# Handing a transformer layer's token mixer over to its mixture of experts: order, places, weight ring and last stage

## The chip, the cores and the metric

One core of one Trainium2 chip runs the whole layer in one launch. The metric is the device time of that launch in microseconds; 1,024 tokens of width 1,024, all in 32-bit floats.

## What is computed

The layer has two halves. The token mixer (differential attention and gated linear attention, then two branch projections and an output projection) is added to its input and normalized. The second half, around which the change lies, is a mixture of 32 experts in 4 groups:

```python
u = _modulate(x, sh2, sc2)
g_idx = argmax(u @ w_rg + b_rg)                    # one of 4 groups per token
top_v, top_i = lax.top_k(e_in, 2)                  # two of its 8 experts
weights = softmax(top_v) * g_w
h = silu(xblk @ wg[e]) * (xblk @ wu[e])            # per expert; 1024 -> 512, twice
yb = h @ wd[e]                                     # 512 -> 1024
y = segment_sum(yb * buf_w)                        # two rows per token, weighted
x = _layer_norm(DEEPNORM_ALPHA * x + g2 * y, ln2_g, ln2_b)
```

## The kernel before

**Router and mixer's end.** `mixer` ends with the output projection of token tiles 4 to 7. For each 128-token tile, `out_tile` (L1550) transposes the residual row, forms the router's logits, and normalizes twice through `norm` (L1524); the second call writes the row that the experts will read, and the logits' last line (L1573) stands behind that call. `Moe.route` and `Moe.forced` (L191) then pick the two experts of each token and, for expert 0 alone, the list of its tokens (`idx` column 0, L205 to L207).

**Three kinds of experts.** Expert 0 is fixed: 128 rows in plain 32-bit, `full32` (L520). The other 31 are sorted by their token counts in `place` (L222): the eight fullest are heavy (`Big`, 256, 192 or 128 rows; each weight half is split by ACT and DVE into two parts, L360 and L361, and multiplied in three terms), the 23 others are light (`Small`, 64 or 32 rows; plain 32-bit weights, no split). `place` gives each token's row position (`posi`, L289), the sorted expert numbers (`eidi`, L249, read by SP as addresses of the weights) and, by 16 matmuls on one-hot tables (L308), the token list of all blocks (`idx`, L309). In the code it stands behind `full32`.

**Weights.** Each expert has six halves of 1 MB (gate, up and down, two each), loaded by SP in order (`load`, L337, L349) into a ring of eight buffers `raw0` to `raw7`. A heavy half leaves its buffer when it is split, a light half when TensorE has multiplied it. The first four ring buffers take the fixed expert's gate and up halves, its down halves go into two spare tiles (L365 to L367). The ring is the first pool on the left side of memory, where the router's constants and the mixer's tiles lay; the pool `pxc`, with the row scales `g2` and the small tables of `place`, is on the right side (L371).

**Order.** `ORDER` (L46) is a string of 140 steps written by hand: H is the next step of the heavy experts (four up steps, a turn, a down step each: 48 steps), L the next one of the light experts (two up steps, the down step of the expert before, a turn: 92 steps). TensorE keeps that order; the splits of a heavy step are issued two steps ahead (L738 to L745). Rows of tokens come by indirect gathers on POOL (`gather`, L388): tag `xg` and tag `xgl` have one buffer each. Before the first step the two row blocks of the first heavy expert are gathered and turned, then the first light expert's (L728 to L732).

**Last stage.** After a loop over overflow blocks (L763, its count is read by every engine) the eight token tiles are finished in the order 4, 5, 6, 7, 0, 1, 2, 3 (L794): two gathers on POOL per tile (`y_rows`, L784, four tiles ahead, 6 buffers each), TensorE adds the two weighted rows through diagonal matrices, tiles 4 to 7 with the residual as a third product by the identity and ACT for the sum (L809), tiles 0 to 3 with the residual added by DVE (L811). Then the mean (L812), ACT's squares (L813), variance (L814), a power on POOL (L815), and two DVE passes (L816, L817) before the store (L818). The residual rows of tiles 0 to 3 are loaded by SP near the end of the steps (L657 to L660).

## Time and profile before

| | |
|---|---|
| Time, median of 3 runs | 2019.95 us (2017.43 to 2022.34) |
| Profiled execution: its time | 2018.9 us |
| its span, first to last instruction | 2017.1 us |
| mean granted TensorE clock | 0.971 |
| PE busy | 1878.1 us (93%) |
| DVE busy | 1154.8 us (57%) |
| ACT busy | 851.0 us (42%) |
| POOL busy | 222.8 us (11%) |
| HBM read, written | 359.64 MB, 72.89 MB |

The span is cut in stages further below. All times of rows are microseconds from the start of the span. PE is TensorE's matmul, DVE is VectorE, ACT is ScalarE, POOL is GpSimd, SP is the engine that issues most loads. L327 is the line of a helper through which all matmuls of the experts go, L330 that of the transposes; the tile names tell them apart (`tru` rows of tokens, `pf` and `ypf` the fixed expert's up and down products, `ptb` the token lists, `pg` and `pu` heavy up, `ps` light up, `yp` down, `fs` the last stage). A 32-bit matmul shows as two records, so counts of its instructions are twice the number in the code.

### The profile page before, as it was taken

How to read it: one execution, taken by the hardware profiler on the slowest of the kernel's cores; microseconds unless marked ns; L12 is line 12 of the kernel's file. 1: busy time of each engine (PE TensorE's matmuls, PEld its weight loads, DVE VectorE, ACT ScalarE, POOL GpSimd, SP SyncE). 2: the span in 40 equal slices, each digit the busy share in tenths (PEclk: the TensorE clock that was granted, in tenths of full speed). 3: DMA queues.
4: the chain of work that ended last, by engine and by line, in shares of the span. 5: the costliest groups of instructions: out<-in, count | busy, mean ns of one | idle time of the engine just before them, and what ended most of it. 6: DMA issues, size and time to landing. Idle time of an engine off the chain costs nothing. (4 is left out here: it accounts for less than half of the span.)

```text
span 2017.1 us, 29004 instructions
## 1 busy us (share of the span) xinstructions
PE 1878.1 (93%) x11019; PEld 1369.9 (68%) x11019; DVE 1154.8 (57%) x2123; ACT 851.0 (42%) x1434; POOL 222.8 (11%) x345
## 2 busy tenths in 40 slices
PE   6999999999999999999998999995989898899886
PEld 4777777777777777777776788884646545466542
DVE  7755276576567655887633576788423324335555
ACT  5321166566557655566563343532212212223422
POOL 1131200000000000000010100101101111011115
PEclk9999999999999999999999999997899999999988
DMA  7896482311221322122158844634799999999976
GB/s 279 227 247 216 137 284 94 102 61 58 95 88 41 102 78 83 45 85 75 58 161 291 262 153 136 207 113 174 301 422 418 410 422 414 421 405 422 396 317 242
DMA packets 142668, 430.59 MB, mean 213 GB/s; under 512 B 20102, under 2 KB 49414, under 8 KB 116416
## 3 DMA queue, kind: packets, MB, share of 16 engines
q1 hardware_dynamic: 99168, 350.60, 47.0%
q0 software_dynamic: 42880, 77.97, 12.1%
q8 instruction: 87, 1.43, 0.3%
q14 instruction: 53, 0.43, 0.1%
q10 hardware_dynamic: 480, 0.16, 0.0%
HBM read 359.64 MB, written 72.89 MB: 214 GB/s over the span
## 5 line engine op out<-in xcount | busy, mean ns | idle before, releaser
L327 PE MATMUL ps<-rawr,xT 128*32 128x256 f32 (+1 forms) x1120 | 133.6, 455 | 15.2 <-DMA rawr<-in_wu 9.3
L1152 DVE CUSTOM_DVE_ANT_0 t<-sc,B 128x256 f32<-128x256 f32 (+7 forms) x128 | 95.8, 754 | 63.8 <-PE sc L1149 58.7
L361 DVE TENSOR_TENSOR wL<-rawr,wH 128x1024 fp32r<-128x1024 f32 x96 | 113.4, 1220 | 19.5 <-ACT wH L360 18.9
L923 PE MATMUL v<-wv,uH 128*128 128x512 f32 x256 | 103.4, 414 | 5.8 <-DVE veL L868 4.5
L327 PEld LDWEIGHTS ps<-rawr,xT 128*32 128x32 f32 (+1 forms) x1120 | 50.2, 119 | 85.1 <-issue 43.9
L1154 ACT ACTIVATE t<-t,nm 128x256 f32<-128x256 f32 (+7 forms) x128 | 98.7, 772 | 17.1 <-DVE nm L1152 16.8
L360 ACT CAST wH<-rawr 128x1024 fp32r<-128x1024 f32 x96 | 95.5, 1048 | 22.7 <-DMA rawr<-in_wd 9.0
L885 PE MATMUL g<-uH,wH_g 128*128 128x512 f32 x256 | 102.3, 400 | 1.8 <-DVE kz L1111 1.8
L574 ACT ACTIVATE sg<-ps 64x256 f32<-64x256 f32 (+1 forms) x23 | 11.0, 479 | 218.6 <-PE ps L327 218.6
L924 PE MATMUL v<-wv,uL 128*128 128x512 f32 x256 | 102.7, 401 | 0.0
L925 PE MATMUL v<-wv,uH 128*128 128x512 f32 x256 | 102.3, 400 | 0.0
L886 PE MATMUL g<-uL,wH_g 128*128 128x512 f32 x256 | 101.9, 398 | 0.0
L887 PE MATMUL g<-uH,wL_g 128*128 128x512 f32 x256 | 101.7, 397 | 0.0
L576 DVE TENSOR_TENSOR h<-ps,sg 64x256 f32<-64x256 f32 (+1 forms) x23 | 12.7, 554 | 115.8 <-ACT sg L574 115.8
L867 ACT CAST aH<-pta 128x512 fp32r<-128x512 f32 (+1 forms) x80 | 43.4, 543 | 71.2 <-PE pta L1173 70.8
L1147 PE MATMUL sc<-sk,sq 128*128 128x512 f32 (+2 forms) x192 | 70.1, 369 | 1.2 <-DVE nm L1152 0.3
L868 DVE TENSOR_TENSOR aL<-pta,aH 128x512 fp32r<-128x512 f32 (+1 forms) x80 | 50.7, 633 | 34.8 <-ACT aH L867 33.8
L1159 DVE SCALAR_TENSOR_TENSOR t<-t,rsum,t 128x128 f32<-128x128 f32 (+3 forms) x64 | 52.2, 816 | 27.3 <-ACT t L1158 27.0
L923 PEld LDWEIGHTS v<-wv,uH 128*128 128x128 f32 x256 | 49.1, 194 | 25.8 <-DVE veL L868 6.7
L1149 PE MATMUL sc<-kz,sq 128*128 128x512 f32 (+2 forms) x192 | 65.8, 349 | 0.0
L327 PE MATMUL yp<-rawr,hT 128*32 128x256 f32 (+1 forms) x560 | 63.6, 450 | 0.9 <-DMA rawr<-in_wd 0.8
L598 POOL DMA_DIRECT2D yd<-ys x66 | 34.2, 525 | 241.7 <-DVE ys L596 168.4
(534 smaller groups left out, 5110.9 us busy)
## 6 DMA issues: line engine op xcount, KB each, us to landing
rawr<-in_wg SPq DMA_DIRECT2D x62, 1024.0 KB, 15.6
rawr<-in_wu SPq DMA_DIRECT2D x62, 1024.0 KB, 12.9
rawr<-in_wd SPq DMA_DIRECT2D x62, 1024.0 KB, 15.0
war<-in_w_ada SPq DMA_DIRECT2D x32, 512.0 KB, 5.8
yd<-o SPq DMA_DIRECT2D x24, 512.0 KB, 6.5
wa<-in_w_ada_sc SPq DMA_DIRECT2D x8, 1024.0 KB, 9.0
wvr<-in_wv SPq DMA_DIRECT2D x32, 256.0 KB, 3.6
wr_g<-in_wgt SPq DMA_DIRECT2D x16, 512.0 KB, 4.7
```

Source lines behind the costliest of these rows:

```text
L327: return tc.keep_in_program_order(nc.tensor.matmul(*a, **kw))
L360: S.copy(H[:, s], raw[:, s])
L361: V.tensor_tensor(L[:, s], raw[:, s], H[:, s].bitcast(F32), op=ALU.subtract)
L885: MM(ps, H[:, k, :], uH[k][:, s], start=k == 0, stop=False)
L886: MM(ps, H[:, k, :], uL[k][:, s], start=False, stop=False)
L887: MM(ps, L[:, k, :], uH[k][:, s], start=False, stop=k == 7)
L923: MM(ps, uH[k][:, t], wv[c][k][:, 0, :], start=k == 0, stop=False)
L924: MM(ps, uL[k][:, t], wv[c][k][:, 0, :], start=False, stop=False)
L925: MM(ps, uH[k][:, t], wv[c][k][:, 1, :], start=False, stop=k == 7)
L1147: mm = MM(ps[:, k0:k1], q, SK[:, c, k0:k1], start=True, stop=False)
L1152: V.tensor_tensor_reduce(out=t[:, :n], in0=ps[:, :n], in1=B[:, 1024 - n:1024], scale=1.0, scalar=3e38, op0=ALU.add, op1=ALU.min, accum_out=nm)
L1154: S.activation(t[:, :n], t[:, :n], AF.Exp, bias=nm, scale=-1.0, accum_out=rsum[:, c:c + 1])
```

## The change

- `ORDER` begins with light steps and ends with three of them; it has the same 48 heavy and 92 light steps.
- `forced` merges the last two small DVE operations into one; `norm` gets a hook, through which the logits' last line is issued ahead of the second pass over the row.
- `place` becomes a generator that is begun before `full32`. Its matmuls for the token lists come out of its middle and are put behind the fixed expert's up products, ahead of its Silu. The sorted numbers (`eqc`, `eid`, `eidi`) move behind `posi`.
- The pool `pxc` becomes the first pool on the left side, and the ring lies behind it. The fixed expert's down halves are loaded after the gather of its rows; a one-element memset on POOL, queued behind the gather, touches each of the two tiles first, and `g2_loads` follows.
- The fixed expert's turned rows are copied by ACT instead of DVE.
- The first light expert's rows are gathered and turned first; the second row block of the first heavy expert is turned at its first step.
- Last stage: all 16 gathers are issued at once into 8 buffers each, the residual rows of tiles 0 to 3 are loaded on POOL's queue behind the first eight gathers; only the first tile takes the residual through TensorE and ACT, the other seven through DVE; the power on POOL becomes a square root on ACT and a reciprocal on DVE.

The moved `eqc` block (L242 to L249 before) stands unchanged behind L289, and `epsf` is a constant column set by a memset.

```diff
-ORDER = ("HHLLHLLLHLLLLHLLLLHLLLLHHLLLLLHHLLLLL"
-         "LLHHLLLLHHLLLLLHHLLLLLLLHHLLLLHHLLLLL"
-         "HHLLLLLLLHHLLLLHHLLLLHHLLLLHHLLLLLHHH"
-         "HLLLLLHHLLHHHHLHHHLLHHHLLLHLH")
+ORDER = ("LLHLLLLLLHHHLLLLLLLHHLLLLLHHLLLLHHL"
+         "LLLLLLHHLLLHHLLLLHHLLLLLLLHHLLLLHHH"
+         "LLLLLLHLLLLHHLLLLLHHHHLLLLLLLHHHLLL"
+         "LLHHHLLHHHLLHHHLLLLLHHHLLHHHHLLHLLL")
...
-        V.tensor_tensor(self.idxf, pf, self.idxf, op=ALU.add)
-        if i1 == 8:
-            V.tensor_scalar(self.idx[:, 0:NF], self.idxf, float(EMPTY), None, op0=ALU.add)
+        if i1 < 8:
+            V.tensor_tensor(self.idxf, pf, self.idxf, op=ALU.add)
+        else:
+            V.scalar_tensor_tensor(self.idx[:, 0:NF], pf, float(EMPTY), self.idxf, op0=ALU.add, op1=ALU.add)
...
         ptb = pps.tile([128, W], F32, tag="tr", name="ptb")
+        ohs = []
         for h in range(2):
             oh = pr.tile([128, 8, 128], F32, tag="xH", name=f"oh{h}", bufs=3)
+            ohs.append(oh)
...
-            for q in range(8):
-                nc.tensor.matmul(ptb, oh[:, q, :], rb[:, 8 * h + q, :], start=h + q == 0, stop=h + q == 8)
-        V.tensor_scalar(self.idx[:, NF:], ptb[:, NF:], float(EMPTY), None, op0=ALU.add)
...
         V.tensor_copy(self.ovei, ove[0:1, :])
+        yield
+        for h in range(2):
+            for q in range(8):
+                self.tc.keep_in_program_order(nc.tensor.matmul(ptb, ohs[h][:, q, :], rb[:, 8 * h + q, :],
+                                                               start=h + q == 0, stop=h + q == 8))
+        V.tensor_scalar(self.idx[:, NF:], ptb[:, NF:], float(EMPTY), None, op0=ALU.add)
+        yield
...
+        pc = wx.enter_context(tc.tile_pool(name="pxc", bufs=1, reuse_waits="tile"))
         praw = wr_.enter_context(tc.tile_pool(name="raw", bufs=1, reuse_waits="tile"))
...
-        def load(e, which, nm, pool=None, halves=(0, 1), fixed={}):
+        def load(e, which, nm, pool=None, halves=(0, 1), fixed={}, touch=False):
...
+                if touch:
+                    nc.gpsimd.memset(raw[0:1, 0:1], 0.0)
...
+        f0 = [load(0, j, "f0") for j in (0, 1)]
         sp = [phl.tile([128, 2048], F32, tag=t, name=f"rawf0s{j}") for j, t in enumerate(("wL", "wH"))]
-        f0 = [load(0, 0, "f0"), load(0, 1, "f0")]
-        f0.append(load(0, 2, "f0", fixed={0: sp[1], 1: sp[0]}))
...
-        def x_small(u, tag, xg=None):
+        def x_small(u, tag, xg=None, copy=V.tensor_copy):
...
-                V.tensor_copy(T[:, s, :], pt)
+                copy(T[:, s, :], pt)
...
-        def full32(raws, T, ydst):
+        def full32(raws, T, ydst, mid):
...
                 ps.append(p)
+            mid()
             h = px.tile([128, 512], F32, tag="sg", name="hf")
...
-        T0 = x_small(0, "xT64", xg0)
+
         with tc.issue_after(self.last_gather.ins):
+            f0.append(load(0, 2, "f0", fixed={0: sp[1], 1: sp[0]}, touch=True))
             g2_loads()
-        full32(f0, T0, yd[0:128, :])
-        self.place(pc, px, ptr)
+        place = self.place(pc, px, ptr)
+        next(place)
+        full32(f0, x_small(0, "xT64", xg0, S.copy), yd[0:128, :], lambda: next(place))
...
             xl2.append(rows)
-            for i in range(0, 4, 2):
-                t = phl.tile([128, 2, 1024], F32, tag="wL", name=f"x1f{i}")
-                nc.sync.dma_start(t, x1d[i * 128:(i + 2) * 128, :].rearrange("(c p) d -> p c d", p=128))
-                xl2.append(t)
...
+        lights[0].fetch()
         fetch(expert(0), 0)
+        lights[0].rows()
         fetch(expert(0), 1, "xgl")
-        for j in range(2):
-            turn_rows(expert(0), j)
-        lights[0].fetch()
+        turn_rows(expert(0), 0)
...
             if i >= 0 and order[i] is not None:
+                if order[i] == 0:
+                    turn_rows(expert(0), 1)
                 hs[order[i]][2]()
...
-                y = pf.tile([128, 1024], F32, tag=f"y{j}", name=f"y{j}_{i}", bufs=6)
+                y = pf.tile([128, 1024], F32, tag=f"y{j}", name=f"y{j}_{i}", bufs=8)
...
+        for i in order:
+            y_rows(i)
+            if i == 7:
+                for q in range(0, 4, 2):
+                    t = phl.tile([128, 2, 1024], F32, tag="wL", name=f"x1f{q}")
+                    nc.gpsimd.dma_start(t, x1d[q * 128:(q + 2) * 128, :].rearrange("(c p) d -> p c d", p=128))
+                    xts[q], xts[q + 1] = t[:, 0], t[:, 1]
         for n, i in enumerate(order):
-            for m in order[n:n + 4] if n == 0 else order[n + 3:n + 4]:
-                y_rows(m)
...
-            if i > 3:
+            if n == 0:
                 terms.insert(0, (ident, xts[i]))
...
-            if i > 3:
+            if n == 0:
                 S.activation(y0, ps, AF.Identity, accum_out=sm[:, 0:1])
...
-            V.tensor_scalar(sm[:, 1:2], sm[:, 1:2], 1.0 / 1024, EPS, op0=ALU.mult, op1=ALU.add)
-            nc.gpsimd.tensor_tensor(sm[:, 2:3], sm[:, 1:2], mhalf, op=ALU.pow)
+            S.activation(sm[:, 2:3], sm[:, 1:2], AF.Sqrt, bias=epsf, scale=1.0 / 1024)
+            V.reciprocal(sm[:, 2:3], sm[:, 2:3])
...
-    def norm(src, dst, tmp, junk, g, b, nmu, sm, acc=None):
+    def norm(src, dst, tmp, junk, g, b, nmu, sm, acc=None, mid=lambda: None):
...
         G.tensor_tensor(sm[:, 1:2], sm[:, 0:1], mhalf, op=ALU.pow)
+        mid()
         V.scalar_tensor_tensor(dst, tmp, sm[:, 1:2], b, op0=ALU.mult, op1=ALU.add, accum_out=acc)
...
-        norm(z, u2, u2, xa, rows["sc2"], rows["sh2"], sm[:, 5:6], sm[:, 6:8])
-        V.scalar_tensor_tensor(lg, lg, sm[:, 7:8], rc[:, 2, :], op0=ALU.mult, op1=ALU.add)
+        norm(z, u2, u2, xa, rows["sc2"], rows["sh2"], sm[:, 5:6], sm[:, 6:8],
+             mid=lambda: V.scalar_tensor_tensor(lg, lg, sm[:, 7:8], rc[:, 2, :], op0=ALU.mult, op1=ALU.add))

```

## Rows read from the trace of the kernel before

**Rows 1.** Windows of stages: length, busy PE, PEld, DVE, ACT, POOL; clock, DMA share, GB/s.

```profile
1320.00:1375.00 55.00, 54.22 (x292) 44.66 (x291) 45.55 (x132) 19.00 (x30) 5.06 (x9) 1.00 0.17 63
...
1475.00:1945.00 470.00, 425.29 (x2666) 260.49 (x2665) 193.94 (x264) 122.67 (x162) 60.90 (x94) 0.96 1.01 414
```

**Rows 2.** Windows of 5 us each, same columns, where the weight stream stands.

```profile
1440.00:1445.00 5.00, 5.00 (x24) 4.10 (x23) 3.10 (x4) 1.91 (x3) 0.66 (x1) 1.00 0.61 184
1445.00:1450.00 5.00, 5.00 (x24) 4.09 (x23) 0.00 (x0) 0.60 (x1) 0.00 (x0) 1.00 0.00 0
1450.00:1455.00 5.00, 4.65 (x74) 2.91 (x72) 1.29 (x2) 0.60 (x1) 0.99 (x1) 1.00 0.31 84
```

**Rows 3.** Timeline of SP, the queue of weight loads: start, length, engine, line, operation.

```profile
1390.07 0.82 SPq L349 DMA_DIRECT2D rawf<-in_wg  x2
...
1427.88 7.11 SPq L349 DMA_DIRECT2D rawr<-in_wu  x2
1453.57 0.33 SPq L349 DMA_DIRECT2D rawr<-in_wg  x1
```

**Rows 4.** Timeline of PE around the fixed expert; in brackets idle time before, and its releaser.

```profile
1401.59 1.94 PE L330 MATMUL tru<-ident,xgu 128*128 128x128 f32 x8 [10.21 <-DMA xgu<-u2d,idx]
1403.46 14.58 PE L327 MATMUL pf<-rawf,xT 128*128 128x512 f32 x32
1420.11 0.66 PE L330 MATMUL trf<-ident,hf 128*128 128x128 f32 x4 [2.07 <-DVE hf L531]
1420.61 5.87 PE L308 MATMUL ptb<-rb,oh 128*128 128x47 f32 x32
1426.27 9.94 PE L327 MATMUL ypf<-rawf0s,hTf 128*128 128x512 f32 x16
...
1451.61 3.66 PE L327 MATMUL ps<-rawr,xT 128*32 128x256 f32 x64 [0.35 <-DVE xT L420]
```

**Rows 5.** Timeline of POOL, the gather of the fixed expert's rows.

```profile
1393.62 1.09 POOL L393 DMA_INDIRECT xgu<-u2d,idx  x1 [6.78 <-DVE idx L207]
```

**Rows 6.** Timeline of DVE: a copy of the fixed expert's rows, and the place step.

```profile
1402.71 0.69 DVE L420 COPY xT<-tru 128x512 f32<-128x512 f32 x1 [4.46 <-PE tru L330]
...
1404.17 1.14 DVE L248 TENSOR_REDUCE eid<-eqc 128x31 f32<-128x961 f32 x1
...
1412.91 0.17 DVE L289 CAST posi<-pos 128x16 int32<-128x16 f32 x1
```

**Rows 7.** Timeline of PE from the last loads on.

```profile
1945.65 1.93 PE L327 MATMUL yp<-rawr,hT 128*32 128x256 f32 x32 [0.18 <-issue]
...
1955.09 0.39 PE L327 MATMUL yp<-wH,hL 128*128 128x512 f32 x1
...
1967.77 5.43 PE L327 MATMUL fs<-y,dg 128*128 128x512 f32 x8 [4.47 <-DMA y<-yd,posi]
...
1985.05 17.33 PE L327 MATMUL fs<-y,dg 128*128 128x512 f32 x40
```

**Rows 8.** Timeline of POOL, the last store and the first gather of result rows.

```profile
1960.03 0.57 POOL L518 DMA_DIRECT2D yd<-ys  x1 [13.31 <-issue]
1963.21 1.05 POOL L788 DMA_INDIRECT y<-yd,posi  x1 [2.61 <-DMA yd<-ys]
```

**Rows 9.** Timeline of DVE: two final tiles and the last instruction.

```profile
2001.17 1.22 DVE L811 SCALAR_TENSOR_TENSOR y<-fs,x1f 128x1024 f32<-128x1024 f32 x1
...
2005.29 1.22 DVE L811 SCALAR_TENSOR_TENSOR y<-fs,x1f 128x1024 f32<-128x1024 f32 x1
...
2011.20 1.29 DVE L817 SCALAR_TENSOR_TENSOR y<-y,sm,l 128x1024 f32<-128x1024 f32 x1 [0.44 <-POOL sm L815]
```

**Rows 10.** Timeline of ACT: a table load, and the stores of the last light expert.

```profile
1384.96 1.28 ACT L214 ACT_TABLE_LOAD   x1
...
1952.07 1.77 ACTq L598 DMA_DIRECT2D yd<-ys  x4
```

**Rows 11.** ACT group of the final stage: operation, tiles, count, busy, mean ns, idle.

```profile
L813 ACT ACTIVATE y<-y,sm 128x1024 f32<-128x1024 f32 x8 | 9.2, 1148 | 14.0 <-DVE sm L812 11.1 <-issue 2.9
```

More of the change, by code (lines that the diff above doesn't have):

```diff
@@ L240, in place @@
         V.tensor_reduce(er, big, axis=AX.X, op=ALU.add)
-        eqc = t([128, NS, NS], "eqc")
-        iN = ii[:, 0:NS]
-        V.tensor_tensor(eqc, er.unsqueeze(1).to_broadcast([128, NS, NS]),
-                        iN.unsqueeze(2).to_broadcast([128, NS, NS]), op=ALU.is_equal)
-        V.tensor_tensor(eqc, eqc, iN.unsqueeze(1).to_broadcast([128, NS, NS]), op=ALU.mult)
-        eid = t([128, NS], "eid")
-        V.tensor_reduce(eid, eqc, axis=AX.X, op=ALU.add)
-        V.tensor_scalar(self.eidi[:, NF:32], eid[0:1, :], float(NF), None, op0=ALU.add)
         cap, base = t([128, 32], "cap"), t([128, 32], "base")
@@ L289, in place @@
         V.tensor_copy(self.posi, pos)
+        eqc = t([128, NS, NS], "eqc")
+        iN = ii[:, 0:NS]
+        V.tensor_tensor(eqc, er.unsqueeze(1).to_broadcast([128, NS, NS]),
+                        iN.unsqueeze(2).to_broadcast([128, NS, NS]), op=ALU.is_equal)
+        V.tensor_tensor(eqc, eqc, iN.unsqueeze(1).to_broadcast([128, NS, NS]), op=ALU.mult)
+        eid = t([128, NS], "eid")
+        V.tensor_reduce(eid, eqc, axis=AX.X, op=ALU.add)
+        V.tensor_scalar(self.eidi[:, NF:32], eid[0:1, :], float(NF), None, op0=ALU.add)
         blk, off = t([128, 8, 2], "blk", I32), t([128, 8, 2], "off", I32)
@@ L362, in split @@
             return [(H[:, k * n:(k + 1) * n], L[:, k * n:(k + 1) * n]) for k in range(2048 // n)]
+        f0 = [load(0, j, "f0") for j in (0, 1)]
         sp = [phl.tile([128, 2048], F32, tag=t, name=f"rawf0s{j}") for j, t in enumerate(("wL", "wH"))]
-        f0 = [load(0, 0, "f0"), load(0, 1, "f0")]
-        f0.append(load(0, 2, "f0", fixed={0: sp[1], 1: sp[0]}))
         px = wx.enter_context(tc.tile_pool(name="px", bufs=2, reuse_waits="tile", side="right"))
         pxs = wx.enter_context(tc.tile_pool(name="pxs", bufs=1, reuse_waits="tile", side="right"))
-        pc = wx.enter_context(tc.tile_pool(name="pxc", bufs=1, reuse_waits="tile", side="right"))
         pgu = wp.enter_context(tc.tile_pool(name="pgu", bufs=4, space=PSUM, reuse_waits="tile"))
@@ L744, in experts @@
             if i >= 0 and order[i] is not None:
+                if order[i] == 0:
+                    turn_rows(expert(0), 1)
                 hs[order[i]][2]()
         xts = dict(self.x1)
-        for i in range(4):
-            xts[i] = xl2[1 + i // 2][:, i % 2]
         lg, lb = xl2[0][:, 0], xl2[0][:, 1]
@@ L791, in y_rows @@
                 ys[i].append(y)
+        epsf = pf.tile([128, 1], F32, name="epsf", bufs=1)
+        V.memset(epsf, EPS)
         pf2 = fin.enter_context(tc.tile_pool(name="finp", bufs=4, space=PSUM, reuse_waits="tile"))
         order = (4, 5, 6, 7, 0, 1, 2, 3)
+        for i in order:
[5 more added lines that the diff above has]
+                    xts[q], xts[q + 1] = t[:, 0], t[:, 1]
         for n, i in enumerate(order):
-            for m in order[n:n + 4] if n == 0 else order[n + 3:n + 4]:
-                y_rows(m)
             y0, y1 = ys[i]
```

## The prediction

> **What bounds the kernel now.** I read the windows by stage first. At the mixer's end TensorE is busy 54.2 of 55 us and DMA 0.17; between 1475 and 1945 DMA is busy throughout (1.01, 414 GB/s) and TensorE 425 of 470 us [rows 1]. So the expert stage is bound by its weights: 186 loads of 1.05 MB, 2.5 us each at that rate. Time is saved there only by having more loads done when the stream becomes dense, or behind the last load. The 5 us windows show where the stream stands: shares of 0.61, 0.00 and 0.31 lose 1.95 + 5 + 3.45 = 10.4 us [rows 2]. SP's timeline says why: two loads leave from 1427.88 on, the next at 1453.57 [rows 3], when the first light expert, whose products start at 1451.61 [rows 4], lets go of a buffer. The ring is full and TensorE does two heavy steps first. Then TensorE's timeline ahead of that: it waits 10.21 us for the fixed expert's rows, gathered at 1393.62 [rows 5] beside the six loads that leave from 1390.07 on [rows 3], then runs pf, a hole of 2.07, trf, ptb, ypf to 1436.2 [rows 4]. Last the tail: the last light down step starts at 1945.65, when the last loads are there; TensorE ends with a heavy down step at 1955.48 [rows 7]; its store leaves at 1960.03, the first result gather at 1963.21 [rows 8], the first weighted product at 1967.77 [rows 7], the last DVE pass ends at 2012.49 [rows 9].
>
> The sum is made against the profiled execution, 2018.9 us, which is 1.05 below the median; that is added at the end.
>
> **(a) The lead of the weight stream.** I follow the chain to the first light step.
>
> *Logits, merged operation.* The logits' last line no longer stands behind a DVE pass of the kind that takes 1.29 [rows 9]; the merged operation saves another of some 0.16 (one-column size, [rows 6]). The row write moves behind one small operation and lands before the gather needs it. I take 1.2; ends 0 and 1.4.
>
> *Gather.* Four of the six loads move into the mixer's end, where DMA is idle [rows 1]; the other two follow the gather. From issue to use the gather now takes 7.97 [rows 4, 5]; two gathers on an emptier DMA take 4.56 [rows 7, 8]. These are the ends; I take 5.1, nearer the second, since only two loads remain beside it. The rows are then turned from 1397.5 instead of 1401.6. The Trainium skill ("DMA: Bandwidth & Descriptors", Queues, rings and completion order) says that each DMA engine goes round-robin, packet by packet, between the queues with work; by that a half-MB gather would be slowed by at most its own moving time, some 1.3 us (an estimate from the rate above), so the early loads would save 1.6 us less than I take. The 7.97 speaks for the longer queue. The memsets on POOL have no row; each costs between nothing and the 1.05 of a POOL issue [rows 8]. Behind them stand the scale loads and SP's two down loads, not needed before ypf, 20 us later: nothing.
>
> *Copies and places.* ACT's copies take about what DVE's 0.69 does [rows 6]: nothing. But DVE no longer waits 4.46 ahead of them [rows 6], so posi comes 4.46 + 1.4 + 1.2 earlier and, without the three passes over 31 x 31 (1.14 each [rows 6]), at about 1402.5. They follow there, so the expert numbers come at about 1406, as now (1405.3, [rows 6]); SP's first loads leave about 2 us later. That is early enough: eight loads and three half-MB gathers need 24 us, and the ring is refilled only at 1436 (below).
>
> *TensorE.* From 1397.5: turning 1.87, pf 14.58, ptb 5.87 right behind it, which covers Silu and the hole of 2.07; trf 0.5; then a wait of about 1.0 for its copy, which ptb hid before; ypf 9.94 [rows 4]. At pf's pace ypf's 16 records would take 7.3; I keep the row's value, since the small ptb products still precede it. End 1431.3 instead of 1436.2. The light expert's gather leaves when ptb is done (1420); now 9.6 pass from ptb's end to the next use [rows 4], so it is covered. Two turns of eight blocks (at most 1.94 each, [rows 4]; I take 2.6 in all) and half of the 3.66 for two steps [rows 4]: the first buffers are free at 1435.7 instead of 1453.5.
>
> *Lead.* By then eight loads are done and the stream has stood some 5 us; it resumes at 1436.7. When the old stream resumes at 1454.6 with ten loads done, the new one has done 8 + 17.9/2.5 = 15.2, less about 2 for a second stand: the next light expert's gather shares its one buffer with the heavy expert's second block, so it leaves only after that block is turned at the first heavy step, and two buffers wait for it. 13.2 - 10 = 3.2 loads: **8 us**. Ends: with no gain ahead of the light step it starts at 1440 and the lead is 2; without the second stand it is 13. After that both orders keep DMA dense, and TensorE's 45 idle us [rows 1] cover the heavy steps.
>
> **(b) Behind the last load.** Now 1955.48 - 1945.65 = 9.83, because a heavy down step stands last [rows 7]. After: the last light down step alone, 1.93 [rows 7]. The heavy one stands three steps earlier; four loads (10 us) still follow its weights, against the 9.83 - 1.93 = 7.9 that it takes now behind the light one. **-7.9**; ends -5 (it doesn't fit whole) and -8.5.
>
> **(c) Store and loop.** Now 7.73 from TensorE's end to the first result gather [rows 7, 8]. After: product 0.5, four issues on ACT's queue 1.77 [rows 10], then the loop's passage, 3.8 now (DVE's product, 0.69 at this size [rows 6], ends about 1956.2, POOL goes on at 1960.03 [rows 8]); the store lands meanwhile. 6.1: **-1.6**; ends 0 and -3. SP's two residual loads go to POOL's queue; SP then waits for nothing there.
>
> **(d) Last stage.** Now 2012.49 - 1963.21 = 49.28. After: 4.56 to the first products, 5.43 for them [rows 7, 8], about 2.5 for ACT's sum and squares (1.15 each [rows 11] and their readings), then DVE, which becomes the bound: 2.9 for tile 4 and seven tiles at the 4.12 of today's last ones [rows 9]: 31.7. TensorE needs 17.33/5 = 3.47 per tile [rows 7], hidden. 16 gathers at 1.05 with gaps of some 0.3 and the two residual loads at 0.57 [rows 8] end about 22 us on, the data 5 us later; TensorE wants the last pair at 34: hidden. No gather waits for a buffer. A square root of one column (less than the 1.15 of a whole row [rows 11]) and a reciprocal replace the power, whose last wait was 0.44 [rows 9]; one table load of 1.28 [rows 10] lies beside DVE's passes over the tile before, and behind the root on ACT stands only the next tile's square pass. 44.2: **-5.1**; ends -2 (DVE idle between tiles) and -7.
>
> **Sum.** -8 - 7.9 - 1.6 - 5.1 = -22.6: 1996.3 profiled, 1997.3 on the median's footing, **1997**. All four at their small ends give -9, at their large ends -31.5.
>
> **Rivals.** *Small lead.* The new memory of the ring may be free no earlier, or the gather may land no sooner; then the first light step comes near 1440 and (a) is 2: 2003. For it: the ring's first buffers must outwait every mixer tile they cover. Against: the weight tiles of the mixer's last projection are the oldest there. 0.18. *Large lead.* No second stand: (a) is 13, 1992. For it: the gathers go ahead of queued loads. 0.15. *Tables.* If ACT's squares were not served while the square root's table is loaded, every tile would pay two loads of 1.28 [rows 10]; with the pass of 1.15, its reading and the root (some 0.5 together) ACT then needs 4.2 a tile, just past DVE's 4.12, and the chain per tile grows: about 3 us lost, 2000. Against: the squares of the last stage show no load although Silu ran before [rows 11]. The Trainium skill ("ScalarE: Activation LUTs", Table sets: the hidden batching unit) puts exp and sqrt in different sets and only cheap functions in every set; it names copy and identity, not the square, and prices a switch at 2.66 us, which would make it some 20 us (an estimate) instead of 3. Its figure for the load alone agrees with the 1.28 here. 0.05. *Dry ring: slower.* SP issues in order, so in runs of heavy steps a light load behind a heavy half that isn't split yet keeps DMA idle, as at 1443 to 1454, at 10.4 us each [rows 2]. The new order starves TensorE with light steps first and bunches heavy ones later. Two such stands eat the gain; three give 1996.3 + 31.2 + 1.05 = 2028.5. Against: TensorE has 45 us to spare and the old order, with runs as long, kept 1.01 for 470 us [rows 1]. 0.07.
>
> **How the numbers follow.** The forecast has 0.55, its own range 1991 to 2003; the rivals have the rest. 1988 to 2008 holds all but the dry ring and corners of the sum. This kernel's measurement tells 0.2%, 4 us, from no change. Faster by more: 0.91; within: 0.03; slower: 0.06.
>
> **What would show it.** Right: four loads of the fixed expert before 1375; pf's start near 1399; `ptb` straight behind `pf`; light products as the first of the steps, near 1434; two short stands instead of one long; a light `yp` as TensorE's last step, about 2 us after the last load; 4.1 us per tile in the last stage, DVE dense, one table load. Wrong: the fixed expert's loads still at 1390; windows below 0.9 DMA share after 1475; a table load per tile; DVE waiting on ACT in the last stage.

## The result, and the profile after

The changed kernel takes 2005.11 us (median of six runs, 1996.58 to 2006.74), the kernel before 2021.54 beside it: a ratio of 0.9901 (0.9884 to 0.9919), taken over all runs (the two medians alone give 0.9919). Faster, by 16 us of the medians; 1997 had been predicted, and 2005 lies in the range of 1988 to 2008 but past the forecast's own end of 2003. The profiled execution takes 2005.35 us, its span is 2003.5, 13.6 less than before.

To compare traces I cut the time behind the mixer at five marks: the fixed expert's gather, load number 36 of the experts' weights leaving SP, the last weight load leaving SP, TensorE's end in the steps, the first gather of result rows, VectorE's end. Each length is a difference of starts or ends in the timelines. (The mixer itself, its code unchanged but for `forced` and `norm`, ends some us earlier or later in each execution: the gather leaves at 1391.6 to 1399.1 us. The cut keeps that out.) Clock is that of the stretch called stream. A load leaves SP when a buffer of the ring comes free, so the second and the third mark tell of buffers, not of landings.

| us | start | stream | clock | behind last load | store | last stage | sum |
|---|---|---|---|---|---|---|---|
| before | 131.0 | 412.6 | 0.96 | 18.2 | 7.7 | 49.3 | 618.9 |
| changed | 118.9 | 420.4 | 0.96 | 14.2 | 9.0 | 42.1 | 604.6 |
| difference | -12.1 | +7.8 | | -4.0 | +1.3 | -7.2 | -14.3 |

So the start gave more than the prediction asked of it, the stream gave two thirds of that back, half of the gain behind the last load came, the store's part changed sign, and the last stage gave more.

Windows of the kernel before and of the changed kernel, from load 36 to the last load and, below the dots, where the stream stands in each (length, busy PE, PEld, DVE, ACT, POOL; clock, DMA share, GB/s):

```profile
1524.65:1937.25 412.60, 376.12 (x2307) 234.54 (x2300) 172.47 (x227) 112.13 (x147) 52.10 (x80) 0.96 1.01 414
...
1770.00:1780.00 10.00, 10.00 (x123) 6.64 (x121) 7.42 (x12) 5.66 (x9) 3.61 (x6) 1.00 0.91 340
...
1890.00:1900.00 10.00, 10.00 (x46) 4.39 (x45) 3.85 (x9) 2.03 (x3) 0.58 (x1) 1.00 0.88 302
```

```profile
1513.85:1934.21 420.36, 382.82 (x2334) 236.81 (x2330) 176.04 (x231) 116.02 (x153) 51.75 (x81) 0.96 1.00 408
...
1425.00:1430.00 5.00, 4.82 (x18) 2.29 (x16) 1.60 (x3) 0.00 (x0) 0.04 (x1) 1.00 0.70 284
1430.00:1435.00 5.00, 4.54 (x74) 2.82 (x72) 2.36 (x4) 1.09 (x2) 2.57 (x3) 1.00 0.71 224
...
1450.00:1455.00 5.00, 5.00 (x24) 1.64 (x22) 2.36 (x2) 1.99 (x2) 0.00 (x0) 0.92 0.51 159
...
1750.00:1760.00 10.00, 10.00 (x76) 4.00 (x76) 3.30 (x8) 3.69 (x7) 1.60 (x2) 1.00 0.89 298
...
1850.00:1860.00 10.00, 7.72 (x62) 3.54 (x58) 5.69 (x8) 5.98 (x9) 3.38 (x5) 1.00 0.92 363
1860.00:1870.00 10.00, 8.71 (x25) 6.55 (x26) 7.14 (x10) 3.38 (x5) 0.11 (x1) 0.66 1.02 424
1870.00:1880.00 10.00, 9.65 (x73) 7.24 (x72) 7.72 (x10) 5.89 (x6) 2.12 (x3) 1.00 0.75 266
```

The long stand of [rows 2], 10.4 us, has become two short ones (0.70 and 0.71, then 0.51: 3 and 2.5 us). DMA stands later on, too: 0.89, 0.92 and 0.75 against the dense 1.01 are 1.2, 0.9 and 2.6 us, and in the first and the last of these stretches TensorE is busy 10 and 9.65 of 10 us. The kernel before has such windows as well (0.91 and 0.88, 1.0 and 1.3 us). Ahead of the 0.75 its clock was 0.66, a mixture of its levels of 2.4 and 1.2 GHz, after 10 us in which it was busy 7.72.

The changed kernel's timeline of SP, against [rows 3]:

```profile
1415.58 0.33 SPq L359 DMA_DIRECT2D rawr<-in_wg  x1
1433.67 0.33 SPq L359 DMA_DIRECT2D rawr<-in_wu  x1
...
1453.21 3.77 SPq L359 DMA_DIRECT2D rawr<-in_wu  x3
...
1513.85 0.33 SPq L359 DMA_DIRECT2D rawr<-in_wu  x1
...
1912.33 6.89 SPq L359 DMA_DIRECT2D rawr<-in_wd  x2
1919.75 0.33 SPq L359 DMA_DIRECT2D rawr<-in_wg  x1
1922.48 0.33 SPq L359 DMA_DIRECT2D rawr<-in_wu  x1
1925.08 9.46 SPq L359 DMA_DIRECT2D rawr<-in_wd  x4
```

of PE, against [rows 4, 7]:

```profile
1398.41 1.94 PE L337 MATMUL tru<-ident,xgu 128*128 128x128 f32 x8 [5.67 <-DMA xgu<-u2d,idx]
1400.17 15.37 PE L334 MATMUL pf<-rawf,xT 128*128 128x512 f32 x32
1415.38 3.67 PE L322 MATMUL ptb<-rb,oh 128*128 128x47 f32 x32
1418.88 0.64 PE L337 MATMUL trf<-ident,hf 128*128 128x128 f32 x4
1420.23 8.70 PE L334 MATMUL ypf<-rawf0s,hTf 128*128 128x512 f32 x16 [0.72 <-issue]
...
1431.71 3.66 PE L334 MATMUL ps<-rawr,xT 128*32 128x256 f32 x64
...
1446.55 1.19 PE L337 MATMUL tru<-ident,xgu 128*128 128x128 f32 x8 [4.40 <-DMA xgu<-u2d,idx]
...
1935.26 0.51 PE L334 MATMUL yp<-wL,hH 128*128 128x512 f32 x1
...
1941.85 3.65 PE L334 MATMUL yp<-rawr,hT 128*64 128x512 f32 x16
...
1946.50 1.93 PE L334 MATMUL yp<-rawr,hT 128*32 128x256 f32 x32 [0.73 <-DVE hT L593]
```

of POOL, against [rows 5, 8]:

```profile
1394.95 1.09 POOL L401 DMA_INDIRECT xgu<-u2d,idx  x1 [6.46 <-DVE xgu L400]
...
1436.89 0.98 POOL L401 DMA_INDIRECT xgu<-u2d,idx  x1 [3.72 <-PE tru L337]
...
1957.43 1.06 POOL L795 DMA_INDIRECT y<-yd,posi  x1 [9.79 <-DMA yd<-ys]
```

and of DVE and then ACT, against [rows 9 to 11]:

```profile
1951.33 0.42 DVE L605 TENSOR_TENSOR ys<-yp,g2q 128x256 f32<-128x256 f32 x1 [4.88 <-DMA yd<-ys]
...
1989.23 1.22 DVE L825 SCALAR_TENSOR_TENSOR y<-fs,x1f 128x1024 f32<-128x1024 f32 x1
...
1992.95 1.22 DVE L825 SCALAR_TENSOR_TENSOR y<-fs,x1f 128x1024 f32<-128x1024 f32 x1
...
1998.25 1.28 DVE L831 SCALAR_TENSOR_TENSOR y<-y,sm,l 128x1024 f32<-128x1024 f32 x1
```

```profile
1951.78 3.68 ACTq L607 DMA_DIRECT2D yd<-ys  x4
...
1970.07 1.28 ACT L828 ACT_TABLE_LOAD   x1
1971.37 0.29 ACT L828 ACTIVATE sm<-sm,epsf 128x1 f32<-128x1 f32 x1
```

What the reader is to see: the light products start at 1431.7 instead of 1451.6 [rows 4]; a second, shorter wait for rows at 1446.55, behind the gather of 1436.89; TensorE's last step is a light down step, as the change wants, but a whole heavy and another light down step stand between the last load (1934.2) and it; and VectorE, which has nothing else to do, waits 4.88 us for a store ahead of the last product, 2.9 of them behind TensorE's end.

### The profile page after: what moved, and what is told of

The parts are those of the page before. It is cut to its first block, busy times and chain, and to the rows that moved or that the text cites. A ratio compares the mean times of both kernels' runs of the same rounds, so it can differ in the third digit from the quotient of the medians.

```text
span 2003.5 us, 28975 instructions
## 1 busy us (share of the span) xinstructions
PE 1873.7 (94%) x11007; PEld 1366.5 (68%) x11007; DVE 1156.0 (58%) x2127; ACT 851.8 (43%) x1439; POOL 211.0 (11%) x341
## 6 DMA issues: line engine op xcount, KB each, us to landing
rawr<-in_wu SPq DMA_DIRECT2D x62, 1024.0 KB, 13.6
```

## The experiments

Ratios are to the kernel before, run beside each; the changed kernel's own are 0.9901 above and 0.9908 in e12. The groups were run at different times (the kernel before takes 2020.1 us beside e1 to e4, 2024.5 beside e5 to e8, 2023.1 beside e9 to e12), so times of different groups are compared by ratio; 0.001 is 2 us. The same five lengths for all, each of a single execution; e5's lies 10.6 us above the median of its runs, e10's 8.1 below:

| us | start | stream | clock | behind last load | store | last stage | sum |
|---|---|---|---|---|---|---|---|
| e1, old last stage | 120.9 | 415.7 | 0.96 | 14.2 | 7.7 | 48.0 | 606.4 |
| e2, old order | 131.4 | 407.8 | 0.97 | 18.2 | 8.7 | 43.1 | 609.2 |
| e3, late fixed expert | 123.8 | 416.8 | 0.96 | 14.2 | 9.0 | 41.9 | 605.6 |
| e4, second buffer | 113.7 | 418.7 | 0.96 | 14.2 | 9.4 | 41.9 | 598.0 |
| e5, last product | 118.4 | 420.0 | 0.95 | 14.2 | 8.1 | 44.1 | 604.8 |
| e6, late places | 125.4 | 416.6 | 0.96 | 14.2 | 10.0 | 41.8 | 607.9 |
| e7, before with last stage | 133.7 | 409.3 | 0.97 | 18.2 | 8.8 | 41.9 | 611.9 |
| e8, two repairs | 116.2 | 412.7 | 0.98 | 14.2 | 7.9 | 44.2 | 595.2 |
| e9, stores first | 119.5 | 416.6 | 0.96 | 14.2 | 6.0 | 42.3 | 598.5 |
| e10, three repairs | 116.5 | 411.0 | 0.98 | 14.2 | 6.3 | 40.8 | 588.8 |
| e11, x1 behind | 119.3 | 413.5 | 0.97 | 14.2 | 7.4 | 41.1 | 595.4 |
| e12, changed again | 118.1 | 419.6 | 0.96 | 14.2 | 9.7 | 42.0 | 603.6 |

### Which part of the change gave what (e1, e2, e3, e6, e7)

**e1** gives the changed kernel the last stage of before, x1 rows on SP included:

```diff
...
-                y = pf.tile([128, 1024], F32, tag=f"y{j}", name=f"y{j}_{i}", bufs=8)
+                y = pf.tile([128, 1024], F32, tag=f"y{j}", name=f"y{j}_{i}", bufs=6)
...
-            if n == 0:
+            if i > 3:
...
-            S.activation(sm[:, 2:3], sm[:, 1:2], AF.Sqrt, bias=epsf, scale=1.0 / 1024)
-            V.reciprocal(sm[:, 2:3], sm[:, 2:3])
+            V.tensor_scalar(sm[:, 1:2], sm[:, 1:2], 1.0 / 1024, EPS, op0=ALU.mult, op1=ALU.add)
+            nc.gpsimd.tensor_tensor(sm[:, 2:3], sm[:, 1:2], mhalf, op=ALU.pow)
...
```

> The changed kernel with the last stage of before (six buffers per gather kind, the power on POOL, tiles 4 to 7 added on TensorE, x1 rows loaded on SP behind the last weights). Theory A: the rebuilt stage alone bought what the profile shows, 49.3 - 42.1 = 7.2 us from its first gather to VectorE's end, whatever stands before it: 2005.1 + 7.2 = 2012 us, with VectorE's period back near 4.1 us. Rival B: part of the 7.2 is paid for by the 2 MB of x1 rows that POOL now loads at 1930 and 1940 us, in the middle of the last weights; putting them back lets the weights land some 3 us earlier: 2009 us, stage 49 us, TensorE's end of the experts some 3 us earlier. Rival C: the stage's length follows the time at which the stores landed, and the old stage here takes as little as the new: 2005 us.

2008.07 us, 0.9932 (0.9907 to 0.9957). The stage is 48.0 long again, 5.9 more, and VectorE waits for POOL's power in each tile:

```profile
1989.15 1.22 DVE L824 SCALAR_TENSOR_TENSOR y<-fs,x1f 128x1024 f32<-128x1024 f32 x1
...
1992.08 1.28 DVE L830 SCALAR_TENSOR_TENSOR y<-y,sm,l 128x1024 f32<-128x1024 f32 x1 [0.38 <-POOL sm L828]
1993.28 1.22 DVE L824 SCALAR_TENSOR_TENSOR y<-fs,x1f 128x1024 f32<-128x1024 f32 x1
```

A period of 4.13 with a wait of 0.38, against 3.72 with none. C falls, the stage is 5.9 us longer; by ratio the loss is 5 to 6 us, between A's and B's, and in the profile the stream was 4.7 shorter and the store part 1.3 shorter. Whether the x1 rows are behind that is for e11.

**e2** puts the old string into `ORDER`, everything else as changed.

```diff
-ORDER = ("LLHLLLLLLHHHLLLLLLLHHLLLLLHHLLLLHHL"
+ORDER = ("HHLLHLLLHLLLLHLLLLHLLLLHHLLLLLHHLLLLL"
...
```

> The changed kernel with the order of steps of before. Theory A: the new order carries the shorter work behind the last load (term b of the prediction, 7.9 us) and the lead of the early start (10 to 11 us at the first hundred loads) stays as it is: 2005.1 + 7 = 2012 us, the last load issued at about the same time (1934 us). Rival B: it is the new order's runs of heavy steps that lose 5 to 6 us of the lead after load 100; with the old order the lead stays near 10 to the last load (issued near 1929 us), and only the difference is left: 2007 us. Rival C: the order matters for nothing, because the stream of loads sets the end by either: 2005 us.

2009.89 us, 0.9945 (0.9925 to 0.9965). Behind the last load 18.2 again, to 0.01 us what it was before. But the lead is not 10 to 11, as A and B had it: it is nothing, 131.4 against 131.0. PE's and SP's timelines show why:

```profile
1436.35 1.94 PE L337 MATMUL tru<-ident,xgu 128*128 128x128 f32 x8 [1.32 <-DMA xgu<-u2d,idx]
1449.86 3.66 PE L334 MATMUL ps<-rawr,xT 128*32 128x256 f32 x64
```

```profile
1418.78 2.60 SPq L359 DMA_DIRECT2D rawr<-in_wu  x2
1451.82 0.34 SPq L359 DMA_DIRECT2D rawr<-in_wg  x1
```

The ring is full by 1421 us, where before it was at 1435 [rows 3] (its gather left 1.2 us later), and then SP stands for 30 us, until the first light step at 1449.9. Early loads and early places alone buy next to nothing: the lead is made when light steps come first as well, and with these each of the two is worth some 5 to 6.5 us of the start (e3, e6). And the old order's stream, 407.8 at a clock of 0.97, is 12.6 us shorter than the changed kernel's at 0.96. So the time is about A's (by ratio 7 to 9 us above the changed kernel), but not in A's way.

**e3** undoes the early loads of the fixed expert by putting its pool back:

```diff
-        pc = wx.enter_context(tc.tile_pool(name="pxc", bufs=1, reuse_waits="tile"))
...
+        pc = wx.enter_context(tc.tile_pool(name="pxc", bufs=1, reuse_waits="tile", side="right"))
```

> The changed kernel with the constants' pool put back beside the others, so that the fixed expert's first two matrices share the router's space again and load late; everything else as changed. Theory A: the early load gives the stream of weights 10 to 11 us at the start, of which 5.6 are left at the last load: 2005.1 + 5.6 = 2011 us. Rival B: the lead is lost on the way in any case, since runs of heavy steps hold the ring's buffers later on: 2006 us. Rival C: all of it arrives: 2016 us. In the trace: load issues against the changed kernel's at index 36 to 96 later by about 8 to 11 us under all three, at index 184 by 5 to 6 (A), 0 to 1 (B), 10 (C).

2005.01 us, 0.9924 (0.9901 to 0.9948): B's time, but by ratio 3 to 5 us above the changed kernel, between B's and A's, with intervals that overlap. The gather's rows come late, as before (SP, POOL and PE):

```profile
1388.27 0.81 SPq L358 DMA_DIRECT2D rawf<-in_wg  x2
1389.14 1.13 SPq L358 DMA_DIRECT2D rawf<-in_wu  x2
```

```profile
1391.81 1.09 POOL L401 DMA_INDIRECT xgu<-u2d,idx  x1 [6.46 <-DVE xgu L400]
```

```profile
1400.43 1.94 PE L337 MATMUL tru<-ident,xgu 128*128 128x128 f32 x8 [10.83 <-DMA xgu<-u2d,idx]
```

8.6 us from gather to use, against 3.5 in the changed kernel. In this execution the start is 4.9 longer, the stream 3.6 shorter; 1.3 us are left at the last load.

**e6** works out the places behind the fixed expert again, and the expert numbers ahead of them (the `eqc` block goes back to its old place, not shown):

```diff
...
+        full32(f0, x_small(0, "xT64", xg0, S.copy), yd[0:128, :], lambda: None)
         next(place)
-        full32(f0, x_small(0, "xT64", xg0, S.copy), yd[0:128, :], lambda: next(place))
+        next(place)
```

> The changed kernel with the places worked out behind the fixed expert's products again, and the experts' numbers ahead of the rest of the places as before; order, early loads and last stage as changed. Theory A: as with the late fixed expert, a delay of the start of 5 to 9 us is mostly worked off by the heavy steps before the last load, and 1 to 2.5 us of it are left: 2007 us, load issues at index 36 later by 5 or more, at index 184 by 1 to 2.5. Rival B: the whole delay arrives, since the stream of loads runs at its full rate from then on: 2012 us. Rival C: the experts' numbers, which come 7 us earlier this way, matter as much, and nothing is lost: 2005 us.

2011.61 us, 0.9940 (0.9923 to 0.9957): B's time, and by ratio 6 to 8 us above the changed kernel. By the trace the start is 6.5 longer (the token lists follow the fixed expert's down products, the light rows wait for them), the stream 3.8 shorter, 2.7 are left at the last load, as A has it, and the sum is 3.3 longer than the changed kernel's. Trace and ratio disagree, so between A and B it stays open.

```profile
1420.94 7.11 PE L334 MATMUL ypf<-rawf0s,hTf 128*128 128x512 f32 x16 [1.04 <-issue]
1427.89 3.67 PE L322 MATMUL ptb<-rb,oh 128*128 128x47 f32 x32
1437.20 3.84 PE L337 MATMUL tru<-ident,xgu 128*128 128x128 f32 x16 [5.65 <-DMA xgu<-u2d,idx]
```

**e7** is the kernel before with the new last stage alone (e1's diff the other way round, on before).

> The kernel of before with the changed kernel's last stage alone (x1 rows on POOL, sixteen gathers in a row, root and reciprocal in place of POOL's power). Theory A: the stage gives the same 6 us here as undoing it cost there (48.0 against 42.1 us in the traces): 0.997 of before, some 2014.5 us where before takes 2020.5. Rival B: the gain hangs on the new order's earlier gathers and is half of that: 2017.5 us. Rival C: behind the old order's last load the x1 rows on POOL come between and take it back: 2020 us.

2016.27 us, 0.9960 (0.9944 to 0.9976). The stage takes 41.9 instead of 49.3 under the old order too; its store part is 1.1 longer. A holds.

### What took part of the gain back (e4, e5, e8 to e12)

**e4** gathers the second block of the first heavy expert into a buffer of the free kind `ys`:

```diff
-            xg = px.tile([128, 1024], F32, tag=tag, name=f"xg{nm}", bufs=1)
+            xg = px.tile([128, 1024], F32, tag=tag, name=f"xg{nm}", bufs=2 if tag == "ys" else 1)
...
-        fetch(expert(0), 1, "xgl")
+        fetch(expert(0), 1, "ys")
```

> The changed kernel with the second block of the first heavy expert gathered into a free buffer of its own, so that the second light expert's gather no longer waits for that block to be turned (1436.9 us) and TensorE does not stand 4.4 us before the turning at 1446.6 us. Theory A: the loads behind it start 4 us earlier and about half of that is left at the last load, as half of the first lead was: 2003 us. Rival B: the later heavy steps set the pace and nothing is left: 2005 us. Rival C: the extra gather runs beside the two others and each lands later, so that the first heavy step starts later: 2006 us or more.

1998.51 us, 0.9887 (0.9865 to 0.9910). The wait of 4.40 us is gone; the second light expert's rows are there when TensorE turns them:

```profile
1441.89 1.04 PE L337 MATMUL tru<-ident,xgu 128*128 128x128 f32 x8
```

The start is 5.2 shorter and this time the stream is no longer for it (1.7 shorter): by the trace all of it arrives. By ratio it is 3 to 4 us, with intervals that overlap the changed kernel's, and e8 against e5 and e10 against e9 give 4 and 2 us for the same edit: between A's half and the whole. C falls, and B is unlikely.

**e5** takes another tile for the last product, **e9** moreover holds its four stores ahead of the overflow loop (the first three lines are in both, the rest is e9's):

```diff
-                ys = px.tile([128, w], F32, tag="ys", name=f"ys{self.r}")
+                last = self.st is not nc.gpsimd
+                ys = px.tile([128, w], F32, tag="ls" if last else "ys", name=f"ys{self.r}")
...
-                    self.st.dma_start(yd[self.p0:self.p0 + n, g * w:g * w + w], ys[g * n:g * n + n, :])
+                    Small.last = self.st.dma_start(yd[self.p0:self.p0 + n, g * w:g * w + w], ys[g * n:g * n + n, :])
...
-        n_ov = nc.values_load(self.novi[0:1, 0:1], min_val=0, max_val=NOV)
+        with tc.issue_after(Small.last.ins):
+            n_ov = nc.values_load(self.novi[0:1, 0:1], min_val=0, max_val=NOV)
```

> The changed kernel with the last light expert's product in a tile of another kind (free by then), so that it no longer waits for one of the two buffers that POOL's stores hold. Theory A: the 4.88 us of VectorE before that product are a wait of which 2.8 us stand behind TensorE's end (1948.43 to 1951.33 us); without it stores and gathers come as much earlier, TensorE's end to first gather falls from 9.0 to about 6.2 us: 2002 us. Rival B: the store behind the overflow loop's events or the store of the heavy expert ends last instead, and the first gather comes no earlier: 2005 us, still 9 us. Rival C: half of it: 2003.5 us.

1999.29 us, 0.9877 (0.9860 to 0.9894), but by its trace the store part is only 0.9 shorter and the sum no better than the changed kernel's. This execution is the slowest of the six (2009.9 us); where the 5 to 6 us lie that the ratio gives, more than any of the theories, it does not show. DVE, ACT and POOL of e5:

```profile
1951.82 0.42 DVE L606 TENSOR_TENSOR ys<-yp,g2q 128x256 f32<-128x256 f32 x1 [2.06 <-PE yp L334]
```

```profile
1955.99 1.78 ACTq L608 DMA_DIRECT2D yd<-ys  x4
```

```profile
1959.83 1.07 POOL L796 DMA_INDIRECT y<-yd,posi  x1 [8.87 <-DMA yd<-ys]
```

The wait for the buffer is gone, the product follows TensorE at once; the stores leave 3.75 us behind it, because in ScalarE's program they now stand behind the loop's branch. That is B's mechanism, though not B's time: a second thing was late right behind the first. (The last stage is 2 us longer in e5 and in e8; why, no run here settles.)

> The changed kernel with the last product's own tile (as in e5) and its four stores kept ahead of the overflow loop on ScalarE's queue. In e5 the product was done at 1952.24 us and the stores left at 1955.99, when the loop was through. Theory A: the stores behind the loop are what took the wait's place; ahead of it they leave within 0.5 us of the product, TensorE's end to first gather falls from 8.1 to about 5 us, and the time to some 1996.5 us (e5: 1999.3). Rival B: the loop's own events end last for POOL in any case, the first gather comes no earlier than 7.5 us behind TensorE's end: 1999 us.

1998.20 us, 0.9881 (0.9857 to 0.9904). Stores and first gather of e9:

```profile
1944.76 2.66 ACTq L608 DMA_DIRECT2D yd<-ys  x4
```

```profile
1950.20 1.06 POOL L797 DMA_INDIRECT y<-yd,posi  x1 [6.77 <-DVE epsf L803]
```

The stores leave 0.04 us behind the product (1944.30 + 0.42), the gather waits for the loop's end alone, and TensorE's end to first gather is 6.0 us. That is A by the trace. The time lies between A's and B's, 5.8 below e12, run beside it, but by ratio no better than e5 (0.9881 and 0.9877): what the second edit adds is shown by the trace alone.

**e8** joins e4's edit and e5's, the last product's tile:

> The changed kernel with both repairs: the second block's own buffer and the last product's own tile. Theory A: they lie in different stretches and add up, 6.6 us (changed to second buffer, from the mixer's end in the traces) and 2.8 us: 1996 us, 0.987 to 0.988 of before. Rival B: the earlier loads make the last product wait no longer than it did anyway, so that only one of the two counts: 1998.5 us.

1995.68 us, 0.9855 (0.9836 to 0.9874): A's time, by ratio even somewhat less; B's 1998.5 lies outside the interval.

**e10** joins e4's edit and both of e9's:

> The changed kernel with all three repairs: the second block's own buffer, the last product's own tile, its stores ahead of the loop. Theory A: the third adds 3 us to the other two, which gave 1995.7 us: 1992.5 us, 0.984 of before. Rival B: the loop's events keep the first gather where it was: 1995.5 us.

1994.39 us, 0.9870 (0.9845 to 0.9895). By time it can't be told from e8, and A's 0.984 lies outside the interval: the third repair's 3 us are not shown. Its trace has the shortest sum of all, 588.8, but it is that of the fastest of its five runs. By ratio both beat the changed kernel by 6 to 11 us and the kernel before by 26 to 29.

**e11** loads the x1 rows on SP behind the last weights, as before did:

```diff
             xl2.append(rows)
+            for q in range(0, 4, 2):
+                t = phl.tile([128, 2, 1024], F32, tag="wL", name=f"x1f{q}")
+                nc.sync.dma_start(t, x1d[q * 128:(q + 2) * 128, :].rearrange("(c p) d -> p c d", p=128))
+                xl2.append(t)
...
```

> The changed kernel with the x1 rows of tiles 0 to 3 loaded on SP behind the last weights, as before, instead of on POOL at 1930 and 1940 us; last stage and order as changed. Theory A: that TensorE's end came 2.7 us earlier with the old last stage lay in the stretch from load 150 on, where the granted clock was 0.83 instead of 0.66, and not in these rows: no difference from the changed kernel that is run beside it, and the landing of the last weights as long (8.5 to 10 us). Rival B: the rows do take the engines from the last weights: TensorE's end and the time 2.5 us earlier than the changed kernel's.

2002.68 us, 0.9902 (0.9880 to 0.9924), against 2004.01 and 0.9908 of e12: no difference that can be told. Behind the last load it takes 14.2 like all others with the new order, so TensorE's end does not wait for the rows on POOL. That is A's by time, though B's 2.5 us would be within the noise; in the traces e11's stream is 6.1 shorter than e12's, at a clock of 0.97 against 0.96.

**e12** is the changed kernel unaltered.

> The changed kernel itself, unaltered, beside the three others. Theory A: its spread of 1996.6 to 2006.7 us is the clock that TensorE is granted in the stream of weights, which takes 416 us from load 36 to load 184 at a mean clock of 0.95 and 408 at 0.97: median 2003 us, and the profiled run's stretch 410 us or less only if its clock there is 0.96 or more. Rival B: the spread is the memory's rate and has nothing to do with the clock: the stretch is anything from 408 to 416 us at any clock.

2004.01 us, 0.9908 (0.9886 to 0.9930). A's median holds. Its stream takes 419.0 from load 36 to load 184 at a clock of 0.96, where A's two numbers would give 412, and 419.6 to the last load. Over all traces with the new order, of kernels that differ ahead of this stretch and behind it, the stretch to the last load goes with the clock: 420.0 at 0.95, 415.7 to 420.4 at 0.96, 413.5 at 0.97, 411.0 and 412.7 at 0.98. That speaks against B. The window of e10 against the changed kernel's first row above:

```profile
1508.14:1919.14 411.00, 374.50 (x2334) 231.06 (x2330) 175.87 (x231) 116.06 (x153) 52.05 (x81) 0.98 1.01 415
```

Which of the two is cause stays open: a lower clock would free buffers later, and a stream that stands would leave TensorE idle, as it was ahead of the 0.66 above. No run here changes one alone.

## Why the prediction was right and where it was wrong

The sign, the bound and the four places were right; the sum was -22.6 and the profile gives -14.3. In part the time lies in its range by luck: the start and the last stage gave 4.1 and 2.1 us more than worked out, the stream, the end behind the last load and the store 7.8, 3.9 and 2.9 less. Without the first two errors the changed kernel would have taken 2011 us.

**(a) -8; measured -12.1 at load 36, -4.4 at the last load.** Up to the first light step the chain went as worked out, or better: rows used 3.5 us behind the gather instead of 5.1 (and below the end of 4.56; see the gather below), `ptb` in 3.67 instead of 5.87 straight behind `pf`, `ypf` in 8.7, first light products at 1431.7, the ring resumed at 1433.7 instead of 1436.7 (38.7 us behind the gather instead of 44.3), then the second stand, behind the very gather that the prediction named. One small step ahead of it failed: the merged list operation and the hook gave 0.2 instead of 1.2 us (from the DVE pass that writes `z`, ahead of the second normalization, to the gather 12.8 us before, 12.6 after), since the gather now waits for the clearing of its tile, where in [rows 5] it waited for the list. The step that failed is "After that both orders keep DMA dense, and TensorE's 45 idle us [rows 1] cover the heavy steps." In the profiled execution they don't: the ring is full, SP waits up to 14.4 and 11.0 us for a light step's products (before 1754 and 1852) and 10.2 for the split of a heavy half (before 1876), and DMA stands at 1750 to 1760, 1850 to 1860 and 1870 to 1880. The stream costs 7.8 us more.

Load 176 divides this in two. From there to the last load the new order takes 27.6 to 28.4 us in its eleven traces, the old one 24.4 to 26.2 in three: 1 to 4 us, in every execution (2.2 in the profiled one), are the order's. From load 36 to load 176 the new order takes 383.3 (e10) to 392.0 us (the changed kernel), the old one 383.4 to 386.4. So the other 5.6 us of the profiled execution needn't be lost: they go with the clock, and what makes them is as open as in e12. By their traces e3's and e6's delays of 4.9 and 6.5 us at the start shrink to 1.3 and 2.7, and e4's gain of 5.2 arrives whole; by ratio 3 to 5, 6 to 8 and 3 to 4 us arrive. How much of a lead is lost, single traces with streams of 411.0 to 420.4 us can't tell.

The stands are the mechanism of the rival called dry ring, in a milder form: windows below 0.9 DMA share after 1475 as it foresaw, but stands of 1 to 3 us, not of 10.4. As a sign of being wrong such a window does not serve: the kernel before has one, too (0.88).

**The gather.** e3 also decides what was set against the 7.97 us of [rows 4, 5]: with the four early halves queued at 1388.3 to 1390.3 ahead of it, the gather of 1391.81 is used at 1400.43; without them, 3.5 us after its issue. So they cost it 5.2. But this gather is not of half a MB: of its 128 rows the DMA packets of the trace move ten, of 4,096 bytes each (the sixteen gathers of the last stage move all their 2,048), since its other places hold no token (their index, 2,048, lies out of bounds). The 4.56 of a whole gather was therefore no lower end for it. The Trainium skill ("DMA: Bandwidth & Descriptors", Queues, rings and completion order) has each DMA engine go round-robin, packet by packet, over the queues with work. The prediction's estimate from this, at most 1.3 us, is refuted by the 5.2; the rule itself is not, for in e3 the ten rows move 5.0 to 6.5 us behind the issue, between packets of the four halves, and have landed by 8.5; in the changed kernel the first moves 1.8 us behind the issue. What the wait ahead of them is made of, no run here shows.

**(b) -7.9; measured -4.0.** The end that I held for the smallest was -5. The stretch is 18.2 us in every run with the old order and 14.2 in every run with the new one, so it is the order's alone, whatever happens elsewhere. The failed step is that four loads (10 us) still follow the heavy step's weights and so hide it. Six did follow (one gate, one up and four down halves behind the two of 1912.33), but TensorE was behind: it starts the heavy down step at 1935.26, 1 us after the last load left SP, and then has 6.6 us of it, 3.65 of a light one, a turn and 1.93 to do, dense but for 0.73. Its own work, not the last load's landing, ends the stage; I had taken TensorE for the faster of the two up to the end. And the 4.0 are read from the mark of a buffer's coming free: from load 176 to TensorE's end the new order takes 41.8 to 42.6 us, the old one 42.6 to 44.4, so that much of what the order gives behind the last load it takes ahead of it.

**(c) -1.6; measured +1.3.** The predicted passage of the loop is right: e9, with nothing else late, takes 6.0 against the 6.1 worked out, if in other shares (the four issues 2.66 instead of 1.77, the loop behind them 2.8 instead of 3.8). What I missed was ahead of it. Three down steps stand close together now, their products go to two `ys` buffers, and POOL's stores hold both, so the last product waits for a landing [4.88 <-DMA yd<-ys]; and half of its stores then queue behind the loop. By the traces taking the first away alone gives 0.9 (e5), both 3.0 (e9); by ratio the two runs are alike.

**(d) -5.1; measured -7.2**, 5.9 undone in e1, 7.4 alone in e7. A mis-sized term: I gave VectorE the 4.12 per tile of [rows 9], which held the wait for POOL's power that the change removes (0.44 in [rows 9], 0.38 per tile in e1). Without it the period is 3.72, and 7 x 0.40 is 2.8, somewhat more than the 2.1 by which the term was missed. The rival about tables falls: one load in the stage (1970.07), squares and roots in turn without another. The Trainium skill ("ScalarE: Activation LUTs", Table sets: the hidden batching unit) names relu, copy, identity and abs as in every set; the trace shows the square to be served beside the root as well.

Of the rivals, small lead and large lead missed on what happens behind load 36: the lead at the start was nearly the large one, though with the second stand, the lead at the end nearer the small one.

## What to carry to other kernels

Where a load stream and an engine are both busy nine tenths of the time, a lead gained early may not be kept: ask which of the two is later in each run of heavy steps, and don't take one bound for the whole stage. Cut a trace at more than one mark: where a mark is a buffer's coming free, a gain can move from one stretch to its neighbour. And ask how many rows a gather really moves. Steps drawn together at the end share buffers and store queues that were far apart before, so follow the last product through its buffer, its store's place in the queue and the loop behind it. A per-tile period read from a trace includes the waits that the change removes; take those out before it is used.

## What the runs showed of the hardware that had not been expected

With the same steps, the stretch from load 36 to the last load took 411.0 to 420.4 us, the longer the lower TensorE's granted clock was (0.98 to 0.95). Whether that also makes most of the 10 us by which single runs of the changed kernel differ is not shown, as only two of its runs have a trace (420.4 and 419.6 us). The work behind the last load, in contrast, repeated to 0.05 us in eleven executions. And an indirect gather of ten rows was used 3.5 us after its issue with no load queued ahead of it, and 8.6 after it behind four loads of another queue.
